# A feed-forward written as one list of weight jobs, with rolling load buffers, a delayed down projection, and block sums shared between HBM and VectorE

## The chip, the cores and the metric

The kernel runs on one core of one Trainium2 chip. The metric is the device time of one execution, in microseconds (us). The engines are named as in the profile: PE is TensorE, DVE is VectorE, ACT is ScalarE, POOL is GpSimd, SP is SyncE, which here only issues transfers.

## What is computed

Two layers of a decoder trunk work on 512 positions of width 1024, in float32: a short gated convolution, then a sliding-window attention, each followed by a feed-forward of width 2816.

```
for l in range(2):
    if l == 0:
        h = h + rmsnorm(short_conv_mixer(rmsnorm(h, g0), w_in, conv_w, w_out), g1)
    else:
        # q, k with partial rotary; window 128; one sink per head
        h = h + rmsnorm(attention(rmsnorm(h, g2) @ w_q, k_sh, v_sh, sinks) @ w_o, g3)
    g, u = split(rmsnorm(h, g4[l]) @ w_gate_up[l], 2)      # 1024 x 5632
    h = h + rmsnorm((silu(g) * u) @ w_down[l], g5[l])      # 2816 x 1024
```

## The kernel before

**Arithmetic.** Each float32 operand is split into a high part, rounded to the type that PE takes, and a low part, the difference. A product is three matmuls (`mm3`, L171 to L174: high x low, high x high, low x high). A weight tile is 128 x 1024 elements, 0.5 MB. `split_weights` (L154 to L168) fetches it into a buffer `raw` over SP's queue (`fetch`, L136 to L141), copies it to `whi` on ACT (L167) and subtracts on DVE for `wlo` (L168). There are 5 buffers for `raw` and 5 pairs for `whi` and `wlo` (N_RAW and N_W, L39), 43 half-width slots and 14 wide buffers for activations, and 8 PSUM banks in three pools.

**Stages.** The convolution's three projections run over eight column tiles (`f`, from L514). The out projection is one pass for the left half of the columns (`first_half`, L546) and one for the right half (`second_half`, L597), where `Update` (L212) collects, norms and adds to the residual, and `Ahead` (L362) fetches the next stage's first weights. Then come layer 0's feed-forward, keys and values, the attention in an order written out by hand (`ORDER`, L31 to L33, with rotary steps on POOL in `rope` and `rope_split`, L970 to L983), its out projection, and layer 1's feed-forward.

**Feed-forward** (`ffn`, L685). The 22 column chunks of 128 go in four rounds (`ROUNDS`, L23: 0 to 5, 6 to 9, 10 to 13, 14 to 21). Chunks 0 to 3 are plain: chunks 0 and 1 in `project_first`, 2 and 3 one weight tile each for gate and for up. The other 18 chunks are nine pairs, q = 0 to 8. A pair is one 2 x 2 block product done with seven block products instead of eight (`gate_seven`, L729), in the order 1, 2, 6, 5, 7, 3, 4. Each is one weight tile, 2 halves x 4 depth tiles x 3 matmuls of 256 columns, into the banks `gx`, `gy`, `gz`. Between them ACT and DVE empty or combine the banks (`take`, L746 to L759), and ACT applies silu (L756).

Of the seven weight tiles three are plain blocks of the weights and four are sums of blocks. These sums are made in HBM by transfers that POOL issues and that add to their destination (`Sums`, L396; issued at L408): per pair four copies, then two, one and one additions, 512 KB each. `sum_on` (L433) starts a pair's four steps in turn; in the feed-forward each step waits for an instruction of ACT in a pair before it.

A finished pair's activations are combined for the down projection (`pair_sums`, L708: ACT L716, DVE L717 and L720, then three splits on ACT and DVE L725). After each of the first three rounds comes the down projection of its chunks, again by seven products (`seven`, L791). It fetches all of its `w_dn` blocks first. Its own block differences are subtractions on DVE in the `raw` buffer (L820), then come the splits (L824 on ACT, L825 on DVE), prepared three ahead (`SEVEN_LEAD`). A product is 2 chunks x 2 x 3 matmuls of 512 columns into `px`, `py`, `pz`, which ACT or DVE adds to `mix` (L861). The last round's activations are split only (`pair_acts`, L776 to L780), and its down projection is plain, by `first_half` and `second_half`, into the banks `pmix`.

The kernel is written for a scheduler, but the parts under `tc.manual_schedule` keep their written order on each engine. SP's queue issues a fetch when its buffer is free, in the written order.

Of the kernel before, what the change touches and what calls it, by code (L numbers as in the profile page):

```python
# [10 lines left out]
F32 = mybir.dt.float32  # L11
F32R = mybir.dt.float32r
# [4 lines left out]
P = 128  # L17
D = 1024
# [6 lines left out]
PLAIN = 4  # L25
WARM = 8
LEAD = 2
SEVEN_LEAD = 3
# [10 lines left out]
N_SLOT, N_WIDE, N_RAW, N_W = 43, 14, 5, 5  # L39
# [17 lines left out]
def yoco_kernel(  # L57
# [337 lines left out]

    class Sums:  # L396

        def __init__(self, l, q):  # L400
            self.a = [w_gb[l, q, b] for b in range(4)]
            self.s = [hbm.tile([P, D], F32, name=name("hsum")) for _ in range(4)]
            self.steps = [self.first, self.second, self.third, self.fourth]

        def move(self, dst, src, behind, **kw):
            dst, src = (a.rearrange("(a b) c -> a (b c)", b=2) for a in (dst, src))
            made = tc.keep_in_program_order(
                nc.gpsimd.dma_start(dst, src, max_dma_last_dim=8 * D, **kw))  # L408
            if behind is not None:
                tc.add_manual_dep(made.ins, behind.ins.name, mybir.DependencyInfo(  # L410
                    mybir.DependencyClass.Sync, mybir.DependencyReason.DATA), reason="pace")

        def first(self, behind):
            a11, a12, a21, a22 = self.a
            for s, a in zip(self.s, (a21, a11, a11, a12)):
                self.move(s, a, behind)

        def second(self, behind):
            a11, a12, a21, a22 = self.a
            self.move(self.s[0], a22, behind, accum_op=ALU.add)  # L420
            self.move(self.s[1], a21, behind, accum_op=ALU.add)

        def third(self, behind):
            self.move(self.s[2], self.s[0], behind, accum_op=ALU.add)

        def fourth(self, behind):
            self.move(self.s[3], self.s[2], behind, accum_op=ALU.add)

    sums_of = {(l, q): Sums(l, q) for l in range(2) for q in range((NF - PLAIN) // 2)}
    to_sum = [sums_of[k] for k in sorted(sums_of)]  # L430
    summing = []

    def sum_on(behind=None, more=True):  # L433

        if more and to_sum:
            summing.append(to_sum.pop(0))
        for x in summing:
            x.steps.pop(0)(behind)
        summing[:] = [x for x in summing if x.steps]
# [74 lines left out]
    for f in range(KT):  # L514
# [27 lines left out]
        if 1 <= f < KT - 1:  # L542
            sum_on(more=f % 2)


    def first_half(load, x, n, take, ws1=None):  # L546

        ws = [load(0, j) for j in range(n // 2)]
        raws = [fetch(load(1, j, True)) for j in range(min(2, n // 2))]
        ws1 = []  # L550

        def more():
            if len(ws1) < n // 2:
                ws1.append(split_weights(None, raws.pop(0), True))
                j = len(ws1) + len(raws)
                if j < n // 2:
                    raws.append(fetch(load(1, j, True)))
# [113 lines left out]
    def load_out(half, j, raw=False):  # L671
        src = w_out[half, j]
        return src if raw else split_weights(src)
# [4 lines left out]

    ws1 = first_half(load_out, ys, KT, take_out)
    ahead = Ahead(first_weights(0))  # L680
# [4 lines left out]
    def ffn(l, before, ahead, gain, gpres, following):  # L685
# [5 lines left out]
        def gate_pair(pg, pu):  # L691
# [6 lines left out]
            self_paced.append(nc.scalar.activation(gr, pg, AF.Silu))  # L698
# [5 lines left out]
            pair_sums(gr)  # L704

        self_paced = []

        def pair_sums(gr):  # L708
# [7 lines left out]
            nc.scalar.activation(h, a11, AF.Copy)  # L716
            nc.vector.tensor_tensor(out=lo, in0=a11, in1=h.bitcast(F32), op=ALU.subtract)  # L717
            for o, x, y, op in ((s1, a21, a22, ALU.add), (s2, s1, a11, ALU.subtract),
                                (s3, a11, a21, ALU.subtract), (s4, a12, s2, ALU.subtract)):
                nc.vector.tensor_tensor(out=o, in0=x, in1=y, op=op)  # L720
            t = [(e[:, :256], e[:, 256:])]
            for src in (*sums, gr[:, S:]):
                h, lo = slot("ahi", F32R), slot("alo", F32R)
                nc.scalar.activation(h, src, AF.Copy)
                nc.vector.tensor_tensor(out=lo, in0=src, in1=h.bitcast(F32), op=ALU.subtract)  # L725
                t.append((h, lo))
            acts.append(t)

        def gate_seven(q, factors, out):  # L729
# [3 lines left out]
            a, s = sums_of[l, q].a, sums_of[l, q].s  # L733
            srcs = {1: a[0], 2: a[1], 4: a[3], 5: s[0], 6: s[2], 7: s[1], 3: s[3]}
            chain = {1: "X", 6: "X", 7: "X", 4: "X", 5: "Z", 3: "Z", 2: "Y"}
            pools = {"X": ps_mm, "Y": ps_pt, "Z": ps_sc}
            banks = {}
            gr = wide("gr")
            kept = [slot("st") for _ in range(2)]

            def take(p, e):
                x, y, z = (banks[c][e][:, :256] if c in banks else None for c in "XYZ")
                g0, g1 = (gr[:, c : c + 256] for c in (e * S, e * S + 256))
# [9 lines left out]
                elif p == 3:  # L753
                    nc.vector.tensor_tensor(out=g1, in0=z, in1=s, op=ALU.add)  # L754
                    both = gr[:, e * S : (e + 1) * S]
                    self_paced.append(nc.scalar.activation(both, both, AF.Silu))  # L756
# [5 lines left out]
            for p in (1, 2, 6, 5, 7, 3, 4):  # L762
                whi, wlo = split_weights(srcs[p])
                c = chain[p]
                opened = c not in banks
                if opened:
                    banks[c] = [bank("g" + c.lower(), pools[c]) for _ in range(2)]
                for e in range(2):
                    for k in range(4):
                        kk = slice(e * S + k * P, e * S + (k + 1) * P)  # L770
                        mm3(banks[c][e][:, :256], whi[:, kk], wlo[:, kk], *factors[p][k],
                            opened and k == 0, k == 3 and p in (2, 3, 4), skip_group_check=True)
                    take(p, e)
            out(gr)

        def pair_acts(gr):  # L776
            for c in (0, S):
# [4 lines left out]
                acts.append((hi, lo))  # L782
# [8 lines left out]
        def seven(kps, acts, first):  # L791
# [3 lines left out]
            raw = {}  # L795
            for b in range(4):
                for c, ks in enumerate(cs):
                    if len(ks) > 1:
                        raw[b, c] = fetch(w_dn[l, kps[ks[0]] : kps[ks[-1]] + 1, b])
                    else:  # L800
                        raw[b, c] = slot("raw")
                        nc.sync.dma_start(raw[b, c], w_dn[l, kps[ks[0]], b])

            factor = {1: (0, None), 5: (0, 1), 6: (0, 2), 3: (2, None), 7: (1, 2), 2: (3, None),
                      4: (0, 3)}
            jobs = [(p, c) for p in (1, 5) for c in range(len(cs))]
            jobs.sort(key=lambda j: j[1])
            jobs += [(p, c) for p in (6, 3, 7, 2, 4) for c in range(len(cs))]
            ready, banks, left_of = {}, {}, {p: len(cs) for p in factor}
# [5 lines left out]
            def prepare(p, c):  # L815
                b, other = factor[p]
                n = S * len(cs[c])
                w = raw[b, c][:, :n]
                if other is not None:
                    nc.vector.tensor_tensor(out=w, in0=raw[other, c][:, :n], in1=w,  # L820
                                            op=ALU.subtract)
                hi = wsp.tile([P, D], F32R, tag="whi", name=name("whi"))
                lo = wsp.tile([P, D], F32R, tag="wlo", name=name("wlo"))
                nc.scalar.activation(hi[:, :n], w, AF.Copy)  # L824
                nc.vector.tensor_tensor(out=lo[:, :n], in0=w, in1=hi[:, :n].bitcast(F32),  # L825
                                        op=ALU.subtract)
                ready[p, c] = hi, lo

            for j in range(min(SEVEN_LEAD, len(jobs))):
                prepare(*jobs[j])  # L830
            for j, (p, c) in enumerate(jobs):
                if j + SEVEN_LEAD < len(jobs):
                    prepare(*jobs[j + SEVEN_LEAD])
                bs = chain[p]
                if bs not in banks:
                    banks[bs] = [bank("p" + bs.lower(), pools[bs]) for _ in range(2)]
                    opened = True
                else:
                    opened = False
                hi, lo = ready.pop((p, c))  # L840
                left_of[p] -= 1
                for n, k in enumerate(cs[c]):
                    kk = slice(n * S, (n + 1) * S)
                    for r in range(2):
# [4 lines left out]
                if left_of[p]:  # L849
                    continue  # L850
# [34 lines left out]
        for i in (0, 2):  # L885
            gate_pair(*pss[i : i + 2])
# [484 lines left out]
```

## Time and profile before

| | us |
|---|---|
| median of 3 runs (1086.6, 1084.23, 1087.57) | 1086.6 |
| the profiled execution, its own time | 1089.31 |
| its span, first to last instruction | 1087.5 |
| mean granted clock of PE over the span | 0.984 |

The profile is of one execution. In it "busy" is the time in which an engine has at least one instruction under way, `x` counts instructions, and a name after `L` is a line of the kernel. The rows of `hsum` are the block sums in HBM, by the queue that POOL issues to:

```
hsum<-in_w_gb_dram POOLq DMA_DIRECT2D x108, 512.0 KB, 11.7
raw<-hsum SPq DMA_DIRECT2D x72, 512.0 KB, 4.7
raw<-in_w_gb_dram SPq DMA_DIRECT2D x54, 512.0 KB, 7.2
hsum<-hsum POOLq DMA_DIRECT2D x36, 512.0 KB, 6.5
```

The last number is the median time from issue to landing, in us. A stage is found by its banks: `gx`, `gy`, `gz`, `px`, `py`, `pz` belong to gate pairs and down rounds of the feed-forward, `pmix` to a plain down or out projection.

### The profile page before, as it was taken

The page shows a single profiled execution, that of the slowest core. Times are in us where ns is not written, and L with a number is a line of the kernel's source. Part 1 is how long each engine was busy: PE and PEld are TensorE (multiplying, and loading weights), DVE is VectorE, ACT ScalarE, POOL GpSimd, SP SyncE. Part 2 cuts the span into 40 slices and gives each one's busy share as a digit, 9 for nine tenths or more (in the row PEclk, how much of TensorE's full clock was granted, in tenths as well). Part 3 has the DMA queues.
Part 4 walks back from the last instruction along what each step waited for, and adds up shares of the span by engine and source line. Part 5 has one row for each costly group of instructions (what it writes and reads, how often), then busy time and mean ns, then how long its engine had stood idle before and what let it go on. Part 6 is the DMA issues. An engine that isn't in the chain of part 4 may idle for free.

```text
span 1087.5 us, 17067 instructions
## 1 busy us (share of the span) xinstructions
PE 1049.0 (96%) x6556; PEld 940.4 (86%) x6556; DVE 766.5 (70%) x1294; ACT 552.8 (51%) x1000; POOL 172.2 (16%) x227
## 2 busy tenths in 40 slices
PE   9999999999998988999999999999999989989997
PEld 7888888998997977999798888898979879789986
DVE  5765555779677776664678998778786866956654
ACT  6322235845552534553475776677466444445531
POOL 0332201012021110121021541020211101200001
PEclk9999999999999899999999999999999999989999
DMA  9577753287779779899712123325797797878621
GB/s 334 176 209 235 215 191 118 78 270 196 250 219 291 243 219 317 297 309 308 255 44 75 40 79 98 108 107 139 232 275 206 229 332 253 228 249 247 204 99 78
DMA packets 58482, 218.87 MB, mean 201 GB/s; under 512 B 7200, under 2 KB 8096, under 8 KB 49184
## 3 DMA queue, kind: packets, MB, share of 16 engines
q1 hardware_dynamic: 46304, 141.62, 36.8%
q0 software_dynamic: 11520, 75.51, 26.9%
q8 instruction: 51, 0.84, 0.3%
q10 hardware_dynamic: 576, 0.66, 0.2%
q14 instruction: 31, 0.25, 0.1%
HBM read 211.46 MB, written 81.79 MB: 270 GB/s over the span
## 4 chain that ended last, share of the span: by engine, by line
PE 67%; DVE 13%; DMA 13%; ACT 4%; issue 3%; POOL 0%; POOLq 0%; DVEq 0%; SPq 0%; ACTq 0%
DMA raw<-in_w_dn_dram 7%; DMA raw<-hsum 5%; PE gx L172 4%; PE gx L173 4%; PE gx L174 4%; PE pmix L172 3%; PE pmix L173 3%; PE pmix L174 3%; PE pgu L172 3%; PE pgu L173 3%; PE pgu L174 3%; DVE wlo L825 3%; PE gz L172 2%; PE gz L173 2%; PE gz L174 2%
## 5 line engine op out<-in xcount | busy, mean ns | idle before, releaser
L168 DVE TENSOR_TENSOR wlo<-raw,whi 128x1024 fp32r<-128x1024 f32 x168 | 215.0, 1282 | 116.2 <-ACT whi L167 116.1
L167 ACT ACTIVATE whi<-raw 128x1024 fp32r<-128x1024 f32 x168 | 176.9, 1056 | 199.1 <-PE gx L173 44.2
L172 PE MATMUL gx<-xt,whi 128*128 128x256 f32 x432 | 126.5, 293 | 17.6 <-ACT st L746 17.1
L173 PE MATMUL gx<-xt,whi 128*128 128x256 f32 x432 | 125.6, 291 | 0.0
L174 PE MATMUL gx<-xt,wlo 128*128 128x256 f32 x432 | 125.6, 291 | 0.0
L172 PEld LDWEIGHTS gx<-xt,whi 128*128 128x128 f32 x432 | 86.4, 200 | 18.7 <-ACT st L746 17.9
L408 POOL DMA_DIRECT2D hsum<-hsum x36 | 28.6, 854 | 435.4 <-ACT gr L756 265.5
L173 PEld LDWEIGHTS gx<-xt,whi 128*128 128x128 f32 x432 | 86.5, 200 | 0.0
L174 PEld LDWEIGHTS gx<-xt,wlo 128*128 128x128 f32 x432 | 86.5, 200 | 0.0
L408 POOL DMA_DIRECT2D hsum<-in_w_gb_dram x108 | 71.8, 1051 | 71.5 <-ACT gr L756 39.4
L824 ACT ACTIVATE whi<-raw 128x1024 fp32r<-128x1024 f32 (+1 forms) x56 | 52.0, 949 | 57.7 <-DVE raw L820 44.8
L825 DVE TENSOR_TENSOR wlo<-raw,whi 128x1024 fp32r<-128x1024 f32 (+1 forms) x56 | 60.2, 1087 | 18.7 <-ACT whi L824 18.6
L172 PE MATMUL pgu<-xlo,whi 128*128 128x256 f32 (+1 forms) x192 | 61.6, 321 | 0.0
L173 PE MATMUL pgu<-xhi,whi 128*128 128x256 f32 (+1 forms) x192 | 61.1, 318 | 0.0
L174 PE MATMUL pgu<-xhi,wlo 128*128 128x256 f32 (+1 forms) x192 | 61.1, 318 | 0.0
L172 PE MATMUL pmix<-wlo,ahi 128*128 128x512 f32 (+1 forms) x136 | 52.3, 385 | 1.9 <-DVE wlo L162 1.9
L173 PE MATMUL pmix<-whi,ahi 128*128 128x512 f32 (+1 forms) x136 | 51.9, 382 | 0.0
L174 PE MATMUL pmix<-whi,alo 128*128 128x512 f32 (+1 forms) x136 | 51.7, 380 | 0.0
L756 ACT ACTIVATE gr<-gr 128x512 f32<-128x512 f32 x36 | 22.5, 625 | 46.7 <-DVE gr L754 46.5
L820 DVE TENSOR_TENSOR raw<-raw,raw 128x1024 f32<-128x1024 f32 (+1 forms) x32 | 34.8, 1088 | 11.4 <-DMA raw<-in_w_dn_dram 10.9
L172 PE MATMUL gz<-xt,whi 128*128 128x256 f32 x144 | 41.1, 286 | 0.0
L173 PE MATMUL gz<-xt,whi 128*128 128x256 f32 x144 | 41.0, 285 | 0.0
(279 smaller groups left out, 3167.3 us busy)
## 6 DMA issues: line engine op xcount, KB each, us to landing
hsum<-in_w_gb_dram POOLq DMA_DIRECT2D x108, 512.0 KB, 11.7
raw<-hsum SPq DMA_DIRECT2D x72, 512.0 KB, 4.7
raw<-in_w_gb_dram SPq DMA_DIRECT2D x54, 512.0 KB, 7.2
raw<-in_w_dn_dram SPq DMA_DIRECT2D x40, 512.0 KB, 9.0
hsum<-hsum POOLq DMA_DIRECT2D x36, 512.0 KB, 6.5
raw<-in_w_in_dram SPq DMA_DIRECT2D x21, 512.0 KB, 7.2
raw<-in_w_gu_dram SPq DMA_DIRECT2D x16, 512.0 KB, 3.6
raw<-in_w_out_dram SPq DMA_DIRECT2D x8, 512.0 KB, 5.9
```

What stands on the lines that cost most here:

```text
L167: nc.scalar.activation(hi, raw, AF.Copy)
L168: nc.vector.tensor_tensor(out=lo, in0=raw, in1=hi.bitcast(F32), op=ALU.subtract)
L172: nc.tensor.matmul(out, whi, xlo, start=start, stop=False, **kw)
L173: nc.tensor.matmul(out, whi, xhi, start=False, stop=False, **kw)
L174: nc.tensor.matmul(out, wlo, xhi, start=False, stop=stop, **kw)
L408: nc.gpsimd.dma_start(dst, src, max_dma_last_dim=8 * D, **kw))
L756: self_paced.append(nc.scalar.activation(both, both, AF.Silu))
L820: nc.vector.tensor_tensor(out=w, in0=raw[other, c][:, :n], in1=w, op=ALU.subtract)
L824: nc.scalar.activation(hi[:, :n], w, AF.Copy)
L825: nc.vector.tensor_tensor(out=lo[:, :n], in0=w, in1=hi[:, :n].bitcast(F32), op=ALU.subtract)
```

## The change

1. **One list.** Everything in the feed-forward from chunk 2 to the last pair, and the first weights of the last plain down product, becomes a list of `Job`s, one weight tile each: plain 2, plain 3, gates 0 and 1, down 0, gates 2 and 3, down 1, gates 4 and 5, down 2, gates 6, 7 and 8, closing. The function `in_line` runs it in written order on all engines. The split of a job is written three jobs ahead. Raw buffers go from 5 to 7, and a buffer is fetched again when its last job has been prepared; `whi` and `wlo` go from 5 pairs to 4.
2. **Down a pair late.** In the list, the down round that belongs after gate 0 comes after gate 1, and so on. The activations of the pair before are prepared in six pieces, one after each job.
3. **Sums of down blocks in HBM.** The four differences of the down blocks, before on DVE, are now sums in HBM like the gate's (signs are taken up where the banks are added to `mix`). Blocks of `w_dn` are laid out anew, so that a round's block is one stretch.
4. **Two of a gate's four sums on DVE.** In eight of the nine pairs (`ADDED`, all but q = 5) only two sums are made in HBM; the other two are additions on DVE in place in the raw buffer (`Job.add`), 16 per layer.
5. **When sums start.** A table (`BEGIN`, given twice, the second holds) names the point at which each sum starts: layer 0's from the convolution to gate 2, layer 1's from the start of the attention to gate 2 of layer 1. Within the list, POOL issues 1 + (number waiting) // 6 of the transfers per job, behind the ACT split of the job that is three ahead.
6. **Around it.** `first_half` takes the depth tiles in three groups and fetches up to three weights of the second half ahead instead of two; the convolution fetches three weights at its start instead of two; the factors of the gate (`before.factors()`) are made after the first plain job.

POOL's transfers go from 144 to 128. The instructions per engine go, in program order, from 1285 to 1279 on DVE, 871 to 849 on ACT, and stay at 6491 on PE.

```diff
+ADDED = (0, 1, 2, 3, 4, 6, 7, 8)
+
+BEGIN = {
+    "c0": "g00", "c2": "g01", "c4": "d00", "c6": "g02", "o0": "g03", "o1": "d01", "0f1": "g04",
+    "0f3": "g05", "0p0": "d02", "0p1": "g06", "0s0": "g07", "0p2": "g08",
+    "a0": "g10", "a2": "g11", "a3": "d10", "a5": "g12", "a6": "g13", "a8": "d11", "1f0": "g14",
+    "1f2": "g15", "1p0": "d12", "1p1": "g16", "1s0": "g17", "1p2": "g18",
+}
...
-N_SLOT, N_WIDE, N_RAW, N_W = 43, 14, 5, 5
+N_SLOT, N_WIDE, N_RAW, N_W = 43, 14, 7, 4
...
+        def add(self):
+            if self.make:
+                raw = self.raws[0].tile
+                nc.vector.tensor_tensor(out=raw, in0=raw, in1=self.raws[1].tile, op=ALU.add)
+
+        def prepare(self):
+            if not self.raws:
+                return
+            n = self.raws[0].n
+            raw = self.raws[0].tile[:, :n]
+            hi = wsp.tile([P, D], F32R, tag="whi", name=name("whi"))
+            lo = wsp.tile([P, D], F32R, tag="wlo", name=name("wlo"))
+            self.begun = nc.scalar.activation(hi[:, :n], raw, AF.Copy)
+            nc.vector.tensor_tensor(out=lo[:, :n], in0=raw, in1=hi[:, :n].bitcast(F32),
+                                    op=ALU.subtract)
+            self.w = hi, lo
+
+    def in_line(jobs, late):
+
+        raws = []
+        for j, job in enumerate(jobs):
+            for raw in job.raws:
+                if raw not in raws:
+                    raws.append(raw)
+                raw.last = j
+        n = [0]
+
+        def prepare(j):
+
+            if 0 <= j < len(jobs):
+                jobs[j].prepare()
+            while n[0] < len(raws) and (n[0] < N_RAW or raws[n[0] - N_RAW].last <= j):
+                raws[n[0]].fetch()
+                n[0] += 1
+            if j + 1 < len(jobs):
+                jobs[j + 1].add()
+
+        for j in range(-1, LINE_LEAD):
+            prepare(j)
+        for j, job in enumerate(jobs):
+            if job.run:
+                job.run(job)
+            prepare(j + LINE_LEAD)
+            if j + LINE_LEAD < len(jobs):
+                issue(1 + len(issues) // 6, jobs[j + LINE_LEAD].begun)
+            if late and not job.alone:
+                late.pop(0)()
+            late += job.then() or [] if job.then else []
...
+        def __init__(self, blocks, shape, every=True):
+            self.blocks = blocks
+            n = 4 if every else 2
+            self.sums = [hbm.tile(shape, F32, name=name("hsum")) for _ in range(n)]
+            a, b, c, d = blocks
+            ab, ac, *rest = self.sums
+            self.steps = [[(ab, a, None), (ac, a, None)], [(ab, b, ALU.add), (ac, c, ALU.add)]]
+            if every:
+                abc, abcd = rest
+                self.steps[0] += [(abc, c, None), (abcd, d, None)]
+                self.steps += [[(abc, ab, ALU.add)], [(abcd, abc, ALU.add)]]
+
...
+    def sum_on(at):
+
+        issue(len(issues))
+        if at in BEGIN:
+            summing.append(sums_of[BEGIN[at]])
         for x in summing:
-            x.steps.pop(0)(behind)
+            x.step()
         summing[:] = [x for x in summing if x.steps]
...
             for t in range(2):
-                unit(pss[t], t, ws, x, range(n - 2), n)
+                unit(pss[t], t, ws, x, range(n - 4), n)
+            for t in range(2):
+                unit(pss[t], t, ws, x, range(n - 4, n - 2), n)
...
+            parts = [first, lambda: add(s1, s2, a22, a21, a11), lambda: add(s3, s4, a11, a21, a12)]
+            return parts + [lambda src=src: split(src) for src in (*sums, gr[:, S:])]
...
+            sums = sums_of[f"g{l}{q}"]
+            a21, a22, a11, a12 = (Raw(b) for b in sums.blocks)
+            s1, s3, *rest = (Raw(b) for b in sums.sums)
+            raws = {1: [a11], 2: [a12], 5: [s1], 7: [s3], 4: [a22]}
+            if rest:
+                raws[6], raws[3] = ([r] for r in rest)
+            else:
+                raws[6], raws[3] = [a11, s1], [a12, a11]
...
-                if other is not None:
-                    nc.vector.tensor_tensor(out=w, in0=raw[other, c][:, :n], in1=w,
-                                            op=ALU.subtract)
...
+            b12, b11, b22, b21 = sums.blocks
+            t1, t3, t2, t4 = sums.sums
+            factor = {1: b11, 5: t1, 6: t2, 3: b22, 7: t3, 2: b21, 4: t4}
+            if len(cs) == 1:
+                order = [[(p, 0)] for p in (1, 5, 6, 3, 7, 2, 4)]
+            else:
+                order = [[(1, 0)], [(5, 0)], [(1, 1), (5, 1)], [(6, 0)], [(3, 0)],
+                         [(6, 1), (3, 1)], [(7, 0)], [(2, 0)], [(7, 1), (2, 1)], [(4, 0)],
+                         [(4, 1)]]
...
+                        nc.vector.tensor_tensor(out=m, in0=m, in1=banks[bs][r],
+                                                op=ALU.subtract if half else ALU.add)
...
+            for job in jobs[: None if len(cs) == 1 else -6]:
+                job.alone = True
...
+            factors, jobs = {}, []
+            for f in range(2, PLAIN):
+                jobs += gate_plain(f)
+            jobs[0].then = lambda: factors.update(before.factors())
+            behind_one = []
+            for rd, (f0, f1) in enumerate(ROUNDS):
+                last = rd == len(ROUNDS) - 1
+                for f in range(max(f0, PLAIN), f1, 2):
+                    q = (f - PLAIN) // 2
+                    jobs += gate_jobs(q, factors, pair_acts if last else pair_sums, acts[rd],
+                                      lambda q=q: sum_on(f"{l}p{q}"))
+                    if behind_one:
+                        jobs += behind_one.pop()
+                if last:
+                    break
+                down = down_jobs(range(f0 // 2, f1 // 2), acts[rd], rd == 0,
+                                 sums_of[f"d{l}{rd}"],
+                                 lambda rd=rd: sum_on(f"{l}s{rd}"))
+                behind_one.append(down)
             n = f1 - f0
-            if not final:
-                seven(range(f0 // 2, f1 // 2), acts, rd == 0)
-                acts = []
-                continue
-
-            def load(half, j, raw=False):
-                src = w_dn[l, f0 // 2 + j, half : 4 - half : 3 - 2 * half]
-                return src if raw else split_weights(src)
-
-            res = Update(mix, gain, gpres, True)
-            res.load()
-
-            def take_last(t, half, ps):
-                res.take(t, half, ps)
-                res.scale(t, half)
-
-            ws1 = first_half(load, acts, n, take_last)
+
+            def weights(half, j):
+                return w_dn[l, half : 4 - half : 3 - 2 * half, f0 // 2 + j]
+
+            closing = [Job([Raw(weights(0, j))], None) for j in range(n // 2)]
+            in_line(jobs + closing, late)
...
+                if op in "RH":
+                    issue(len(issues) // 2 if op == "R" else len(issues))
+            sum_on(f"a{i + 1}")
```

More of the change, by code (lines that the diff above doesn't have):

```diff
@@ L393, in one, with __init__, fetch @@
             self.lo()
-    class Sums:
[L400 to L406, printed above, removed]
+    class Raw:
+        def __init__(self, *srcs):
+            self.srcs = srcs
+            self.widths = [s.shape[0] * S if len(s.shape) == 3 else D for s in srcs]
+            self.n = sum(self.widths)
+        def fetch(self):
+            self.tile, c = wraw.tile([P, D], F32, tag="raw", name=name("raw")), 0
+            for src, n in zip(self.srcs, self.widths):
+                dst = self.tile[:, c : c + n]
+                if len(src.shape) == 3:
+                    src, dst = (src.rearrange("k p c -> p k c"),
+                                dst.rearrange("p (k c) -> p k c", c=S))
+                nc.sync.dma_start(dst, src)
+                c += n
@@ L409, in move @@
             if behind is not None:
[L410 to L430, printed above, removed]
+                tc.add_manual_dep(
+                    made.ins, behind.ins.name, mybir.DependencyInfo(
+                        mybir.DependencyClass.Sync, mybir.DependencyReason.DATA),
+                    reason="pace")
@@ L829, in seven, with run, products @@
[L829 to L833, printed above, removed]
+            def run(parts):
+                def products(job):
+                    at = 0
+                    for p, c in parts:
+                        product(p, c, *(w[:, at : at + S * len(cs[c])] for w in job.w))
+                        at += S * len(cs[c])
+                return products
```

286 lines of the change are left out of this document (153 added, 133 removed), and 4 rows, old and new, of the table BEGIN.

## The prediction

> **What bounds the kernel now.** I read the page first: its span, its busy shares and its slices.
>
> ```profile
> span 1087.5 us, 17067 instructions
> PE 1049.0 (96%) x6556; PEld 940.4 (86%) x6556; DVE 766.5 (70%) x1294; ACT 552.8 (51%) x1000; POOL 172.2 (16%) x227
> PEclk9999999999999899999999999999999999989999
> DMA  9577753287779779899712123325797797878621
> ```
>
> TensorE (PE) is busy for 96% of the span. The work of an engine that is full can't be shortened by moving other work, and the change leaves the products alone. So the first question is whether 96% is really full. "Busy" counts a matmul's whole flight, and these flights overlap. The pace must therefore be read from starts. I took the single instructions on PE around the first and the last gate product of layer 0's feed-forward, then the table by stage: all of that stretch, its first gate pair alone, and the same stretch of layer 1.
>
> ```profile
> 230.94 0.39 PE L172 MATMUL pgu<-xlo,whi 128*128 128x512 f32 x1
> 231.16 0.39 PE L173 MATMUL pgu<-xhi,whi 128*128 128x512 f32 x1
> 231.39 0.39 PE L174 MATMUL pgu<-xhi,wlo 128*128 128x512 f32 x1
> 231.62 0.28 PE L172 MATMUL gx<-xlo,whi 128*128 128x256 f32 x1
> 502.01 0.28 PE L173 MATMUL gx<-xt,whi 128*128 128x256 f32 x1
> 502.13 0.28 PE L174 MATMUL gx<-xt,wlo 128*128 128x256 f32 x1
> ```
> ```profile
> 231.62:502.25 270.63, 256.73 (x1808) 241.28 (x1806) 195.06 (x277) 133.57 (x197) 39.17 (x61) 0.97 0.86 268
> 231.62:251.77 20.15, 20.15 (x170) 20.15 (x168) 16.80 (x26) 10.52 (x17) 1.29 (x3) 1.00 0.69 252
> 502.25:548.62 46.37, 44.43 (x188) 35.79 (x187) 28.82 (x44) 21.93 (x38) 7.09 (x9) 0.96 0.82 264
> 766.75:1036.45 269.70, 256.65 (x1808) 241.35 (x1806) 198.97 (x283) 136.82 (x200) 29.11 (x44) 0.97 0.80 247
> ```
>
> The columns are the window, its length, the busy time of PE, weight load, VectorE (DVE), ScalarE (ACT) and GpSimd (POOL), then the granted clock, the DMA share and GB/s. An undisturbed 256-column matmul starts 0.12 us after the one before (502.01 to 502.13), a 512-column one 0.22 to 0.23 us (230.94, 231.16, 231.39; I take 0.23). A gate pair has 7 products x 8 x 3 = 168 matmuls of 256 columns, 168 x 0.12 = 20.2 us, and the first pair took 20.15: it ran at that pace. By the loops in the code the stretch has 9 pairs, 1512 matmuls x 0.12 = 181.4 us, and 7 down pairs x 7 products x 2 x 3 = 294 matmuls x 0.23 = 67.6 us: **249.0 us needed, 270.63 and 269.70 used**. So 21.6 and 20.7 us per layer are not TensorE's work, though PE reads 95% busy; the clock of 0.97 against 1.00 in the first pair says the same.
>
> Where do these 42 us lie? I asked PE's waits in layer 0's stretch, then the worst place in the chain of waits and on ACT.
>
> ```profile
> PE gx L172 <- ACT st L746: 8.9, 2, 4.9
> PE px L172 <- ACT a L716: 2.1, 2, 1.5
> PE px L174 <- DVE a L717: 1.4, 2, 0.7
> ```
> ```profile
> 305.08 12.57 DMA raw<-in_w_dn_dram
> ...
> 339.04 13.95 DMA raw<-hsum
> ```
> ```profile
> 353.08 1.06 ACT L167 ACTIVATE whi<-raw 128x1024 fp32r<-128x1024 f32 x1 [4.59 <-DMA raw<-hsum]
> 354.05 0.36 ACT L746 ACTIVATE st<-gx 128x256 f32<-128x256 f32 x1
> ```
> ```profile
> 345.00:356.00 11.00, 6.08 (x45) 5.87 (x45) 4.84 (x6) 3.97 (x6) 0.00 (x0) 0.90 1.02 315
> 418.00:431.00 13.00, 9.04 (x65) 8.84 (x64) 6.67 (x8) 5.70 (x8) 0.00 (x0) 0.87 0.98 322
> ```
>
> The two waits of nearly 5 us are each the first gate after a down round. PE waits for ACT to empty the bank (`st`), but ACT itself stood behind a split that waited for a weight: `raw<-hsum` took 13.95 us. The down round holds its blocks in the raw buffers until its subtractions are done, so the next gate's loads start together, late, while the DMA engines are full (share 1.02 and 0.98). The round begins with the mirror image, `raw<-in_w_dn_dram`, 12.57 us, and with PE waiting for activations made only just before (`a`). These rows are 12.4 of the 21.6 us; the rest is what shorter waits and a lower clock behind them leave. **The bound is weight delivery at the joints between gate and down, not PE.**
>
> **The change, part by part.**
>
> 1. *Rolling loads.* Raws become 7 single buffers, refilled in the order of use, each tile split 3 jobs ahead of its product. A job is 24 matmuls of 256 (2.9 us) or 12 of 512 (2.8 us), so a load is issued at least 4 jobs, some 11 us, ahead of its split. That alone is a little under the 13.95 us above, but those were loads in a jam. The loads themselves fit: per layer a gate fetches 5 blocks instead of 7 in 8 of 9 pairs (63 to 47 blocks of 0.5 MB), down 12.25 MB instead of 7: about 36 MB in 249 us, 145 GB/s, where the joint moved 315. I take the two kinds of wait as gone.
>
> 2. *Down one pair late.* The activations of a round are split piece by piece during the next gate, so `px` finds them ready: the 2.1 and 1.4 us go. What is late next is DVE, below.
>
> 3. *Sums.* Gate sums by DMA fall from 4 to 2 in 8 of 9 pairs; the down blocks' four sums are new there. POOL's DMA issues go from 144 to 128, the sums of layer 1 start during attention. For them:
>
> ```profile
> 571.00:735.00 164.00, 163.59 (x1070) 140.66 (x1070) 138.68 (x381) 112.92 (x304) 39.90 (x32) 1.00 0.25 84
> POOL sh L975 <- DVE sh L972: 54.6, 8, 24.2
> L408 POOL DMA_DIRECT2D hsum<-in_w_gb_dram x108 | 71.8, 1051 | 71.5 <-ACT gr L756 39.4 <-DMA hsum<-in_w_gb_dram 29.9 <-issue 2.2
> ```
>
> The attention uses 0.25 of the DMA engines, so there is room. About 20 issues land between the rope operations, at most 4 on one tile: 4 x 1.05 = 4.2 us, beside 54.6 / 8 = 6.8 us for which POOL waits before a tile. Cost 0; without that cover, 20 x 1.05 = 21 us at most. A gain could only be in the feed-forward, counted above.
>
> On this the Trainium skill, page "SBUF — State Buffer", section "Who interferes with whom", speaks against the change: `tensor_scalar` can run on VectorE in a mode that holds a port pair shared with GpSimd, and GpSimd then blocks for the whole instruction, descriptors of its own DMAs included. No run here has such DMAs beside the attention's tensor_scalars, so the trace neither shows nor excludes it; by the rule the sum would lie between ours and that of rival D.
>
> 4. *VectorE.* This is what could be late next.
>
> ```profile
> L820 DVE TENSOR_TENSOR raw<-raw,raw 128x1024 f32<-128x1024 f32 x24 | 29.3, 1221 | 11.2 <-DMA raw<-in_w_dn_dram 10.9
> L820 DVE TENSOR_TENSOR raw<-raw,raw 128x512 f32<-128x512 f32 x8 | 5.5, 690 | 0.2
> L825 DVE TENSOR_TENSOR wlo<-raw,whi 128x1024 fp32r<-128x1024 f32 x42 | 51.2, 1220 | 15.2 <-ACT whi L824 15.2
> 320.77 1.14 DVE raw L820
> DVE wlo L168 <- ACT whi L167: 48.5, 41, 4.4
> DVE wlo L825 <- ACT whi L824: 9.3, 8, 2.6
> ```
>
> Removed per layer: 12 x 1.14 + 4 x 0.63 = 16.2 us of subtractions (1.14 from back-to-back starts, as at 320.77; the rows' 1221 ns overlap; 0.63 my estimate for the 690 in that ratio), and three splits (28 to 25 tiles) x 1.2 = 3.6. Added: 2 x 8 adds of the same shape x 1.14 = 18.2. So 195.06 and 198.97 become 193.5 and 197.4; **I take 198, 80% of 249**. DVE's waits for ACT in its splits are now 48.5 + 9.3 = 57.8 us; if all of them stayed, DVE would need 198 + 58 = 256, 7 us more than PE. They don't all stay: a DVE that is behind finds `whi` ready, and the worst of them (4.4) stood behind the late loads. Bounds 0 and 7 per layer; I take 3, nearer the first since a backlog feeds on these waits.
>
> 5. *ACT, SP and the rest.* ACT loses 22 instructions; it has 133.57 of 270 us busy. Weight buffers go from 5 to 4: a tile's buffer is refilled while PE works on the tile before next, 2.8 us for 1.06 + 1.2 of splits. The last round's plain down product follows from 502.25 to 548.62. Its first weights are now split among the jobs, and a third weight is fetched ahead for its second half:
>
> ```profile
> L172 PE MATMUL pmix<-wlo,ahi 128*128 128x512 f32 x62 | 25.1, 405 | 1.9 <-DVE wlo L162 1.9
> ```
>
> 3 x 62 = 186 matmuls x 0.23 = 42.8 needed, 46.37 used, 3.6 to win. In layer 1 the same product ends in the output; I leave it. The conv's sums are as many as before: 0, covered by a POOL that is 16% busy.
>
> **The sum.** 1087.5 - 21.6 - 20.7 - 3.6 + 2 x 3 = 1047.6 us span. The profiled execution took 1089.31, 1.8 over its span: 1049.4. It lay 2.7 above the median of the runs (1086.6): **1047 us** as a median.
>
> **The rivals.**
>
> *Partial (B).* DVE and ACT meet in a written-out order, and their hand-overs leave 9 to 18 us per layer instead of 3: 1047 + 12 to 1047 + 30, that is 1059 to 1077. For it: 80% of DVE, and today's window of a down round, where DVE and not PE is full:
>
> ```profile
> 320.00:345.00 25.00, 23.24 (x112) 18.53 (x112) 24.37 (x38) 11.06 (x14) 6.78 (x10) 1.00 0.81 228
> ```
>
> Against it: this window holds four subtraction pairs and the activations at once, which the change spreads.
>
> *GpSimd held up in attention (D).* The 20 issues, or the rope behind them, lose their cover: 1047 + up to 21 = 1068. For it: the rope sits between DVE and PE. Against: PE is busy 163.59 of 164 us there, so the rope has a lead to eat first.
>
> *Slower (C).* Lockstep: each of 88 splits in a stretch (63 gate, 25 down) is queued on ACT and DVE at the same place, behind the same bank's emptying. If DVE each time arrives just as ACT starts, it waits ACT's whole 1.06 us: 198 + 88 x 1.06 = 291 us against 270 now, +21 per layer: 1087.5 + 42 - 3.6 - 0.9 = **1125**. It decides from 198 + 72 = 270, that is 0.82 us of wait for each split; now it is 57.8 / 89 = 0.65, most of it idle that costs nothing: the first gate pair has 20.15 - 16.80 = 3.35 us of DVE idle and PE doesn't stop.
>
> *The change moves the stalls (E).* The joints' loads are as late as before, since the 7 buffers include some held over a gate for the sums: 1087. Against: the held ones are two of five in a gate.
>
> **How the numbers follow.** Forecast (A), 1037 to 1058: 0.60. B, 1059 to 1077: 0.18. D: 0.05. C: 0.13. E: 0.04. A's low end is no DVE residue, 1041, and 0.225 us for each of 2 x 294 + 186 matmuls of 512, 4 less; its high end is the bound of 7 per layer, 1055, and the 3.6 not won. The range 1037 to 1076 holds A, D and most of B: 0.8. This kernel's measurement can tell about 0.3% from no change: 1083.3 to 1089.9. Faster by more: 0.82 (A, B, D less a tail). Within: 0.04. Slower: 0.14.
>
> **What would show it.** The gate-and-down stretch falls to some 252 us per layer at a clock of 1.00; no `gx <- ACT st` wait near 5 us; no `raw` transfer in the chain of waits within the stretch; the DMA share there falls below 0.7 and rises in attention; DVE shows 32 adds of about 1.2 us and some 80% busy. If PE's waits name `wlo` or a bank that DVE empties, B or C is right; if a `raw` load ends them, E; if the attention is longer than 164 us with POOL behind `hsum`, D.

## The result, and the profile after

The median went from 1085.41 us (four runs, 1083.85 to 1087.57) to **1046.07 us** (four runs, 1045.97 to 1047.46): a ratio of 0.9639, 95% interval 0.9618 to 0.9660. 1047 was forecast. The profiled execution took 1046.09 us, 1.8 over its span. The profiled execution of before, 1089.31 us, lies 3.9 above its median, so the stretches below differ by more than the medians do.

The page of the changed kernel, the lines that answer to those of before, and the share of each engine in the chain that ended last:

```profile
span 1044.3 us, 16975 instructions
PE 1028.0 (98%) x6556; PEld 929.1 (89%) x6556; DVE 770.6 (74%) x1288; ACT 552.9 (53%) x994; POOL 160.5 (15%) x211
PEclk9999999999999999999999999999999999999997
DMA  9657797367979655357303598935778795543601
PE 93%; DVE 4%; issue 1%; DMA 1%; ACT 1%; POOLq 0%; POOL 0%; ACTq 0%; DVEq 0%
```

The chain of before had this instead, with `raw` loads for nearly all of the DMA:

```profile
PE 67%; DVE 13%; DMA 13%; ACT 4%; issue 3%; POOL 0%; POOLq 0%; DVEq 0%; SPq 0%; ACTq 0%
```

The chain is PE now. PE's waits over the whole span are down to three places, none of them in a feed-forward:

```profile
PE pcub L594 <- ACT whi L585: 1.1, 2, 0.6
PE idle L572 <- DVE mhalf L142: 1.1, 1, 1.1
PE psc L1186 <- DVE nm L1198: 0.3, 1, 0.3
```

The stretches, cut at the same instructions as in the prediction (to the first gate product, gates and downs, the last round's plain down, keys to attention and out projection, and so on to the end):

```profile
0.00:229.69 229.69, 227.55 (x1112) 193.17 (x1113) 143.02 (x195) 97.03 (x158) 47.26 (x65) 1.00 0.71 225
229.69:477.83 248.14, 248.14 (x1808) 236.61 (x1806) 198.66 (x283) 138.36 (x202) 19.31 (x30) 1.00 0.69 220
477.83:520.02 42.19, 42.19 (x188) 34.88 (x187) 27.42 (x40) 19.45 (x35) 3.86 (x5) 1.00 0.56 198
520.02:738.58 218.56, 217.96 (x1431) 190.64 (x1430) 176.86 (x449) 147.74 (x372) 69.30 (x84) 1.00 0.59 169
738.58:986.71 248.13, 248.13 (x1807) 236.61 (x1806) 198.64 (x283) 138.16 (x202) 17.08 (x26) 1.00 0.66 215
986.71:1044.30 57.59, 44.02 (x218) 37.24 (x216) 25.97 (x41) 12.15 (x29) 3.72 (x4) 0.90 0.17 69
```

And the three of before that the prediction did not show:

```profile
0.00:231.62 231.62, 229.52 (x1113) 194.10 (x1114) 141.22 (x199) 98.69 (x162) 42.44 (x57) 1.00 0.61 193
548.62:766.75 218.13, 217.69 (x1431) 190.58 (x1430) 178.56 (x453) 150.23 (x376) 50.64 (x52) 1.00 0.27 85
1036.45:1087.50 51.05, 44.02 (x218) 37.25 (x216) 23.93 (x40) 11.53 (x28) 3.71 (x4) 0.97 0.20 81
```

Stretch by stretch: -1.9, **-22.5**, -4.2, +0.4, **-21.6** and **+6.5**, in sum -43.2 us. In both feed-forwards PE is busy for every microsecond of the stretch. The last line is the surprise. Its PE work is the same 44.02 us; the 6.5 us lie behind the last matmul, and there nothing runs:

```profile
1034.90:1043.50 8.60, 0.00 (x0) 0.00 (x0) 0.00 (x0) 0.00 (x0) 0.00 (x0) 0.50 0.13 49
```

The views leave out instructions that only synchronise. Among the trace's own records of them stands what the end waits for, GpSimd's last drain (start and end in us):

```
before  POOL DRAIN 1081.76 to 1084.68; SP's last drain ahead of the closing barrier 1086.77
after   POOL DRAIN 1032.03 to 1043.52; SP's last drain ahead of the closing barrier 1037.03
```

Before, the output's landing, which SP waits for, ended the execution. Now GpSimd does, 6.5 us later.

### The profile page after: what moved, and what is told of

It is laid out like the page before. It is cut to its first block, busy times and chain, and to the rows that moved or that the text cites. A ratio compares the mean times of both kernels' runs of the same rounds, so it can differ in the third digit from the quotient of the medians.

```text
span 1044.3 us, 16975 instructions
## 1 busy us (share of the span) xinstructions
PE 1028.0 (98%) x6556; PEld 929.1 (89%) x6556; DVE 770.6 (74%) x1288; ACT 552.9 (53%) x994; POOL 160.5 (15%) x211
## 4 chain that ended last, share of the span: by engine, by line
PE 93%; DVE 4%; issue 1%; DMA 1%; ACT 1%; POOLq 0%; POOL 0%; ACTq 0%; DVEq 0%
PE gx L192 7%; PE gx L191 7%; PE gx L190 7%; PE pmix L192 5%; PE pmix L190 5%; PE pmix L191 5%; PE gz L192 3%; PE gz L191 3%; PE gz L190 3%; PE pgu L191 3%; PE pgu L190 3%; PE pgu L192 3%; PE px L190 2%; PE px L191 2%; PE px L192 2%; PE gy L192 2%
## 5 line engine op out<-in xcount | busy, mean ns | idle before, releaser
L455 DVE TENSOR_TENSOR wlo<-raw,whi 128x1024 fp32r<-128x1024 f32 (+1 forms) x188 | 227.7, 1214 | 82.1 <-ACT whi L454 81.9
L454 ACT ACTIVATE whi<-raw 128x1024 fp32r<-128x1024 f32 (+1 forms) x188 | 194.8, 1049 | 90.2 <-DVE raw L445 39.5
L521 POOL DMA_DIRECT2D hsum<-in_w_gb_dram x76 | 51.3, 708 | 141.5 <-ACT whi L454 103.4
L289 POOL TENSOR_TENSOR ur<-uv,mhalf 128x1 f32<-128x1 f32 x15 | 11.6, 776 | 365.5 <-DVE uv L285 365.5
L872 ACT ACTIVATE st<-gx 128x256 f32<-128x256 f32 x72 | 27.6, 383 | 74.3 <-PE gx L192 74.2
L185 ACT ACTIVATE whi<-raw 128x1024 fp32r<-128x1024 f32 x30 | 31.8, 1059 | 65.0 <-PE pu L191 24.4
L186 DVE TENSOR_TENSOR wlo<-raw,whi 128x1024 fp32r<-128x1024 f32 x30 | 49.8, 1667 | 2.9 <-ACT whi L185 2.9
L180 DVE TENSOR_TENSOR wlo<-raw,whi 128x512 fp32r<-128x512 f32 x50 | 33.8, 722 | 12.9 <-ACT whi L179 9.6
L192 PE MATMUL gx<-xhi,wlo 128*128 128x256 f32 x144 | 40.8, 283 | 0.0
L190 PE MATMUL gy<-xlo,whi 128*128 128x256 f32 x144 | 40.8, 283 | 0.0
```

The costliest lines, as they stand in the source:

```text
L180: nc.vector.tensor_tensor(out=lo[:, c], in0=raw[:, c], in1=hi[:, c].bitcast(F32), op=ALU.subtract)
L185: nc.scalar.activation(hi, raw, AF.Copy)
L186: nc.vector.tensor_tensor(out=lo, in0=raw, in1=hi.bitcast(F32), op=ALU.subtract)
L190: nc.tensor.matmul(out, whi, xlo, start=start, stop=False, **kw)
L192: nc.tensor.matmul(out, wlo, xhi, start=False, stop=stop, **kw)
L289: nc.gpsimd.tensor_tensor(out=self.r[:, t : t + 1], in0=self.v[:, t : t + 1], in1=mhalf[:, :1], op=ALU.pow)
```

## The experiments

Each of the first eleven is one profiled execution beside one of the kernel before on the same chip. The changed kernel itself was not run again beside them; runs 7 and 9, which left its time alone, stood on two chips and came within 0.4 us of its median. Six runs of kernel 12 spread over 2.1 us, so less than that is not read, and eleven runs of the kernel before on one chip over 8.3 us (1083.70 to 1091.97), so a difference from a single one of those is good to some 4 us.

**1. All gate sums in HBM again.**

```diff
-ADDED = (0, 1, 2, 3, 4, 6, 7, 8)
+ADDED = ()
```

> All four sums of every gate are made in HBM again; the two additions per gate on VectorE are gone. Everything else is the changed kernel. The gates load 7 blocks instead of 5 and POOL issues 160 transfers instead of 128. Theory (weights came late only because buffers were held through a down round): the rolling buffers can carry the 16 extra blocks per layer too, and the time stays at 1046 within 3 us, VectorE some 36 us less busy. Rival (it is the smaller traffic that made the gain): the transfers are late again, PE waits on a split or on ACT's emptying of a bank, and the time is 1055 to 1070.

Measured 1075.68 us (before: 1087.78). The count in the expectation was off: with the 48 transfers for the down blocks it is 192, not 160. The theory fails. The rival has the sign right, but the time is above its 1055 to 1070, and late weights are less than half of it. The two feed-forward stretches grow by 10.9 and 2.2 us, the start up to the first gate product by 11.7, and the time between the two feed-forward stretches by 9.5; the end is 4.6 shorter, for its drain (runs 8 to 12). In the chain the raw blocks of layer 0's joint take 18 us again, with the DMA engines full:

```profile
269.61 17.76 DMA raw<-in_w_dn_dram
...
289.82 18.09 DMA raw<-in_w_gb_dram
```
```profile
262.00:312.00 50.00, 45.54 (x276) 40.50 (x275) 32.06 (x48) 26.53 (x38) 8.94 (x14) 0.99 1.03 342
```

PE's largest wait, though, is elsewhere, behind the two out projections:

```profile
PE xt L327 <- ACT xn L316: 10.9, 3, 5.0
```

In this program POOL took its work in the written order, and the small `ur` that scales a tile stands behind the transfers, some of which wait for earlier ones. First this kernel, then the changed one:

```profile
174.52 0.77 POOL L521 DMA_DIRECT2D hsum<-in_w_gb_dram  x1 [1.33 <-DMA hsum<-in_w_gb_dram]
175.03 2.27 POOL L521 DMA_DIRECT2D hsum<-in_w_dn_dram  x4
177.06 0.84 POOL L289 TENSOR_TENSOR ur<-uv,mhalf 128x1 f32<-128x1 f32 x1
```
```profile
166.93 0.56 POOL L289 TENSOR_TENSOR ur<-uv,mhalf 128x1 f32<-128x1 f32 x1 [12.74 <-DVE uv L285]
```

What `ur` reads was ready at 168.58 us (`uv`, DVE L285), so POOL started it 8.5 us late; in layer 1 it was 6.1 us (`uv` ready at 701.11, `ur` at 707.23). In the changed kernel POOL had been idle for 12.7 us there. Taking two sums per gate off GpSimd is what leaves that room.

**2. Down at once.** The `behind_one` list goes, and `in_line` does all of `late` ahead of a down round.

```diff
-                    if behind_one:
-                        jobs += behind_one.pop()
...
-                behind_one.append(down)
+                jobs += down
```

> Each down round stands right behind the gate pair that ends its chunks, as before the change; what is left of the activations' preparation is done ahead of it in one go. Everything else is the changed kernel. Theory: six rounds each wait for activations made just before; the kernel before showed 7.5 us of such waits on PE in all and more in a lowered clock behind them, so 1052 to 1062, with PE waits at px and clock dips at the rounds. Rival (the delay is not needed, the loads were all): 1046 within 3 us.

Measured 1054.68 us, in the theory's range and 8.6 us more than the change. Of these, 6.8 are the delay's: each of the two stretches grows by 3.4 us, to 251.5. The other 1.8 lie ahead of the first gate product, within the scatter of that stretch. The waits at `px` came back; the half clock that the theory expected behind them did not (both stretches ran at 1.00):

```profile
PE px L192 <- DVE a L838: 2.2, 4, 0.6
...
PE px L190 <- ACT mix L1004: 1.1, 2, 0.6
```

**3 and 4. The buffers alone, in both orders.**

```diff
-N_SLOT, N_WIDE, N_RAW, N_W = 43, 14, 7, 4
+N_SLOT, N_WIDE, N_RAW, N_W = 43, 14, 5, 5
...
-    later = [fetch(w_in[1, t]) for t in range(min(3, N_RAW - 3))]
+    later = [fetch(w_in[1, t]) for t in range(3)]
...
-        raws = [fetch(load(1, j)) for j in range(min(N_RAW - 4, n // 2))]
+        raws = [fetch(load(1, j)) for j in range(min(3, n // 2))]
```

> The changed kernel with the buffer counts of before: 5 raw buffers and 5 pairs of split buffers (the same memory). The weights that are fetched ahead in the plain products stay at three. Theory: order and rolling are not enough; with 5 buffers, of which a gate's additions hold two, a load is issued only one or two jobs (3 to 6 us) ahead of its split, which is near the 4.4 to 6 us that a load takes, so PE waits behind late splits: 1052 to 1080. Rival (it is only the order of the jobs that counts): 1046 within 3 us.

```diff
-N_SLOT, N_WIDE, N_RAW, N_W = 43, 14, 5, 5
+N_SLOT, N_WIDE, N_RAW, N_W = 43, 14, 7, 4
```

> The kernel before with 7 raw buffers and 4 pairs of split buffers, nothing else. Theory (the joints wait since the down round holds 4 blocks, or more in the first round): with 7 buffers three are left for the next gate, so the four waits of 4 to 5 us behind rounds 2 and 3 go with the half clock behind them; the waits for activations stay: 1060 to 1072. Rival (the DMA engines are full at the joint, whatever the buffers): 1080 to 1087.

Measured 1057.22 and 1050.77 us. The first theory held. The second had the cause right and its size wrong: the time came out 9 us below its 1060 to 1072. The same line also makes the kernel before fetch three weights instead of two at the convolution's start; that stretch ended at 230.64 us, 1.0 earlier. **One line in the kernel before brings 37 us (1087.78 to 1050.77, on one chip), where the whole change brings 39.**

| | 5 raw, 5 split | 7 raw, 4 split |
|---|---|---|
| order of before | 1085.4 (median) | 1050.8 |
| one list | 1057.2 | 1046.1 |

The left upper and the right lower figure are medians, the others single executions. The two remedies are for one illness: each alone takes most of it. The lower row also holds 6 us that have nothing to do with the feed-forward, GpSimd's last drain (runs 8 to 12). Without them it would be about 1051 and 1040 (an estimate), so either remedy alone brings about 35 us and both together about 45. PE's waits in the kernel before with seven buffers, and its stretch of layer 0:

```profile
PE px L172 <- DVE mix L861: 4.8, 4, 1.2
...
PE pz L172 <- DVE wlo L825: 1.0, 2, 0.5
```
```profile
230.64:483.94 253.30, 250.09 (x1808) 236.09 (x1807) 198.34 (x283) 137.41 (x200) 39.75 (x63) 1.00 0.92 287
```

253.3 us instead of 270.6, with the old order, DVE's subtractions and a DMA share of 0.92. So a nearly full DMA cost PE little here once the loads were asked for in time. What is left over the changed kernel is 5.2 us per layer. Named waits for DVE in the down rounds are 3.2 of them in layer 0; the list takes all 5.2.

**5 to 7. How near VectorE is to being the bound.** `Job.add` also does this, for 4, 7 or 2 of a gate's seven jobs:

```diff
+            if self.more:
+                raw = self.raws[0].tile
+                nc.vector.tensor_tensor(out=raw, in0=raw, in1=raw, op=ALU.max)
```

> The changed kernel with four more VectorE operations in each gate pair: the raw tile is replaced by the maximum of itself with itself, which leaves its values as they are, at the price of an addition of that shape (1.14 us). 36 more per layer, 41 us: VectorE's busy time in the gate and down stretch goes from 198.7 to about 240 of 248 us. Theory (VectorE's waits for ScalarE are idle time that a backlog eats): PE keeps its pace, 1046 to 1056. Rival (VectorE and ScalarE wait for each other in the written order, and the 41 us of waits stay): 240 + 41 = 281 us against 248, so 33 more per layer, about 1112.

> The same with the operation before every split of a gate pair, 63 per layer, 72 us: VectorE needs 199 + 72 = 271 us for a stretch in which PE needs 248. Theory: VectorE becomes the bound and loses little beside, some 23 to 30 us per layer, 1092 to 1106. Rival: the waits for ScalarE stay on top, 41 us more per layer, near 1170.

> The changed kernel with two more VectorE operations (maximum of a tile with itself) in each gate pair, 18 per layer, 20.5 us. With four and with seven per pair VectorE ended at 88 to 89 per cent of the stretch and set its length. If it can be filled to 88 per cent whatever the load, it needs 199 + 20.5 = 219 us of work, 219 / 0.885 = 248 us, just PE's own length: 1046 to 1050. If each added operation costs as it did at four per pair (18.6 us for 41 us of work), the price is 9 us per layer, 1064.

Measured 1083.33, 1156.33 and 1045.95 us. Four and seven came out between theory and rival, and two at no price, as 88 per cent foretold. The stretch of layer 0, with two, four and seven (the busy time of DVE is the third behind the length, after PE and PEld):

```profile
229.69:477.83 248.14, 248.14 (x1808) 236.64 (x1807) 218.65 (x300) 136.73 (x204) 19.94 (x30) 1.00 0.70 221
```
```profile
229.76:497.10 267.34, 253.23 (x1808) 237.57 (x1808) 236.13 (x318) 137.25 (x203) 19.95 (x30) 1.00 0.65 204
```
```profile
231.30:533.90 302.60, 267.38 (x1808) 245.14 (x1807) 268.77 (x345) 136.88 (x203) 19.92 (x30) 0.98 0.58 180
```

DVE is busy for 218.65 / 248.14 = 88%, 236.13 / 267.34 = 88% and 268.77 / 302.60 = 89%. With two, PE still set the length; with four and seven DVE did. **In this order, with the additions placed there, DVE is full at 88 to 89%**; beyond it the stretch grows about as DVE's work / 0.88. Why the rest can't be filled was not isolated. The change as it stands is at 198.66 / 248.14 = 80%. The waits for ACT shrink with a backlog but don't vanish: `DVE wlo <- ACT whi` is 41.0 us in the changed kernel's stretch and 28.3 us with four more. PE then waits at `gx`, for a bank that DVE empties:

```profile
PE gx L190 <- DVE st L882: 9.3, 6, 2.3
```

**8 to 12. The drain at the end.** `sum_on` also puts idle copies on GpSimd's list, into memory that nothing reads, at the end of the feed-forward of layer 0, four at each of four points (two points for eight copies); number 9 instead moves layer 1's last sums (`"1p2": "g18"` becomes `"1p4": "g18"`).

```diff
+        if at in MORE:
+            for b in range(4):
+                issues.append((hbm.tile([P, D], F32, name=name("spare")), w_gb[1, 0, b], None))
```

> The changed kernel with 16 more copies of 512 KB within HBM, issued by GpSimd between the feed-forward of layer 0 and the attention, into memory that nothing reads: 144 transfers in all, as in the kernel before, and the last one at the same time as in the changed kernel. It asks what the 6.5 us at the end hang on: the last drain of GpSimd ends 1.96 us after its last operation with 144 transfers (the kernel before, and that with seven buffers), 10.5 us with 128 (three kernels), 5.9 us with 192. If it is the number of transfers, the drain falls to 2 us and the time to 1039 to 1041. If it is the time since the last transfer (85 us, 176 to 180 us and 140 us in the same order), it stays at 10.5 us and the time at 1046.

> The changed kernel with the last gate's sums of layer 1 started two gate pairs later, at the end of pair 4 instead of pair 2; still 128 transfers. The last transfer then lies about 120 us before the final drain instead of 179. If the drain follows the number of transfers, it stays at 10.5 us and the time at 1046. If it follows the time since the last one, it falls to between 2 and 6 us, and the time to 1040 to 1043.

> As the kernel with 16 more copies, but of 128 KB each instead of 512 KB. 144 transfers in all. If the final drain follows the number of transfers, it takes 2 us and the time is 1039 to 1041; if it follows their rows or bytes, it is longer than 2 us.

> 8 more copies of 512 KB, 136 transfers in all. If the drain shrinks step by step with the number of transfers, it takes about 6 us (between 10.5 at 128 and 2.0 at 144) and the time is 1041 to 1043. If it drops at a threshold, it is 2 or 10.5 us. If it grows from a wrap near 128, it is shorter than 2 us.

> The version that the runs point to: the changed kernel with 8 more copies of 128 KB, 136 transfers in all. The final drain should take 1.3 us as with 8 copies of 512 KB, and the output's own landing should end the execution. 1038 to 1042, that is 0.957 of the kernel before (bounds 0.953 to 0.961), against 0.964 for the change as it stands.

Numbers 8 to 11 measured 1039.78, 1046.42, 1041.13 and 1041.64 us. Number 12, timed six times, has a median of 1039.87 us (1039.58 to 1041.66), **0.9565 of the kernel before, interval 0.954 to 0.959**. The drain of numbers 10 and 11 is the one foretold for a count that decides (1.96 us, and less than 2); their times are 1.3 and 1.8 us above number 8, because their first gate product started 1.3 and 1.5 us later, and so don't tell the theories of number 11 apart. From the records of POOL's last drain in all runs, the time from the end of GpSimd's last operation to the end of the drain:

| GpSimd's transfers in the program | kernels | us | us / 0.0823 |
|---|---|---|---|
| 128 | the change, runs 2, 3, 5, 6, 7 and 9 | 10.5 | 128 |
| 136 | 8 of 512 KB, 8 of 128 KB | 1.30 | 16 |
| 144 | before, run 4, 16 of 512 KB, 16 of 128 KB | 1.96 | 24 |
| 192 | run 1 | 5.88 | 71 |

It doesn't hang on the time since the last transfer (the late sum left it at 10.53) or on the bytes, but on the number, and not in proportion. 0.0823 is 10.53 / 128. The four counts fit 0.0823 us for each of 128 transfers and, from 136 on, for each above 120; no count below 128 was run, and what makes the drain fall between 128 and 136 is not shown. The changed kernel's 128 is the worst of the four.

## Why the prediction came out right

1047 was forecast, 1046.1 measured. The direction and the mechanism, late weights at the joints, were right; that the two numbers meet within 1 us is partly luck, with errors of both signs.

- *What PE needs.* 249.0 us per stretch, measured 248.14 and 248.13. This is the number that carried the prediction: starts of single matmuls times the counts in the code, against a "busy" of 95% that hid 21 us.
- *Where it was lost.* "Weight delivery at the joints between gate and down": right, and shown by runs 3 and 4. What the prediction didn't see is that the step "Rolling loads" held two remedies. It gave the gain to rolling and count together; the count alone would have done most of it.
- *Down a pair late.* Waits of 3.5 us per layer were put down to it; taking it back costs 3.4 per layer.
- *Sums at no cost.* Right for this kernel. The rival with GpSimd held up did not come in the attention (218.13 before, 218.56 after). 22 transfers fell between the rope operations, about the 20 forecast, and POOL still waited 50.0 us for DVE there. The rival's mechanism is real, though, behind the out projection, and run 1 shows its price, 8.5 us for one late `ur`. The commonest transfer costs POOL the same in the stretch that holds the attention as in the feed-forward, by these two rows:

```profile
L521 POOL DMA_DIRECT2D hsum<-in_w_gb_dram x23 | 15.5, 719 | 37.5 <-ACT whi L454 16.4 <-ACT a L833 10.7 <-DMA hsum<-in_w_gb_dram 10.5
```
```profile
L521 POOL DMA_DIRECT2D hsum<-in_w_gb_dram x20 | 13.7, 714 | 48.2 <-ACT whi L454 48.0 <-issue 0.2
```

  So the rule of the Trainium skill that was weighed there, page "SBUF — State Buffer", section "Who interferes with whom" (a VectorE operation in a two-port mode shuts GpSimd out), shows no clear effect here: 719 against 714 ns. The rarer transfers differ both ways (`w_dn` 788 against 627 ns, `hsum` 805 against 870), and no run isolates the rule.
- *VectorE.* 198 us were forecast, 198.66 measured. The residue of "3 per layer" was 0: the mis-sized term on this side, 6 us. Rival C, the lockstep, needed waits of 0.82 us per split to decide; the changed kernel has 41.0 / 88 = 0.47. Runs 5 to 7 show how much room was left: DVE is full at 88%, which the change keeps clear of by 20 us per layer. ScalarE lost 6 instructions in the two profiles (1000 to 994), not 22; its busy time, 552.8 and 552.9 us, did not matter.
- *The joint behind the last gate.* 3.6 forecast, 4.2 measured. The start was 1.9 us shorter, which the prediction had at 0; it is near the scatter of that stretch (it ends at 229.55 to 231.49 us among the ten kernels of the new order that leave the loads and buffers as they are).
- *The end.* Nothing was forecast there, and it cost 6.5 us. The step "POOL's DMA issues go from 144 to 128" was costed by what POOL does beside other work; what 128 transfers leave for the drain was in no row that was read.

In sum: 1047.6 - 6 (VectorE) - 1.9 (start) - 1.7 (pace) - 0.6 (joint) + 0.4 (attention) + 6.5 (end) = 1044.3, the span. So the terms that were forecast came out 9.8 us too high, and the drain, which was in no term, hid 6.5 of that. The last step, 2.7 off since the profiled execution of before lay above its median, hid most of the rest: the changed kernel's profiled execution lay on its median (1046.09 against 1046.07). Without the drain (run 12, 1039.87) the forecast would have been 7 us too high, still within its range.

## What to carry to other kernels

Work out what the busiest engine needs from the distance of two starts, stage by stage, since its busy share can hide waits and a lowered clock. Where weights come late, try first how many buffers hold them: here one line of constants was worth 37 us, and the rewriting behind it 5 more, or 11 once the drain at the end was short. Look at the end of the trace as well, at the records that no engine counts as busy.

## What was not expected of the hardware

- GpSimd's final drain takes a time that hangs on how many transfers GpSimd has issued in the program: 10.53 us with 128, and 1.30, 1.96 and 5.88 us with 136, 144 and 192. Eight copies that do nothing made this kernel 6 us faster. What the drain does in that time is open.
- In the trace's clock records the kernel before drops to half the clock seven times between 350 and 965 us, for 3.4 or 6.8 us each (the 0.90 and 0.87 of the two windows in the prediction), each time behind PE waits of about 1 to 5 us; the changed kernel does not once before its last matmul. At half the clock a matmul of a gate starts 0.21 us after the one before, instead of 0.12. In layer 0's stretch PE's waits sum to 13.9 us, and 13.7 us at half the clock lose about 6 more (an estimate from these two distances), together 20 of the 22.5 us that the change won there. So a stall cost more than its own length here.
